# Seven-product feed-forward blocks: another order of the products, of the weight groups and of ScalarE's copies

## The chip, the cores and the metric

The kernel runs on one core of a Trainium2 chip. The metric is the device time of one execution in microseconds; the kernel before is given by the median of three runs. The engines are called as the profile calls them: PE (TensorE, matmuls), PEld (its weight loads), DVE (VectorE), ACT (ScalarE), POOL (GpSimd), and SP, whose queue issues the loads of the weights.

## The reference, cut to what matters

One inference step through two layers; 640 token columns (512 latent, 128 context) share all weights. Each layer is a half-step SwiGLU feed-forward, a mixer of three branches (state-space scan, differential attention, pooling) and a second half-step feed-forward, each with an adaptive norm. The change touches the feed-forwards and, in one point, the preparation of the scan's constants.

```python
def swiglu(h, w_in, w_out):
    a, b = jnp.split(h @ w_in, 2, axis=-1)
    return (jax.nn.silu(a) * b) @ w_out
...
    n = rmsnorm(x, ng[0]) * (1.0 + mod[..., 1, :]) + mod[..., 0, :]
    x = x + 0.5 * mod[..., 2, :] * swiglu(n, lp['w_ffn_in'][0], lp['w_ffn_out'][0])
```

The model width is 1024 (8 tiles of 128), the inner width 2816 (22 tiles).

## The kernel before, in words

Activations lie transposed, features on the partitions, and the 640 columns are two halves h = 0 and 1 of 320. Each float32 operand is split in two rounded parts, hi and lo, and a product is three matmuls (hi x hi, hi x lo, lo x hi). A weight block of 1024 x 128 is loaded raw through SP's queue into one of three buffers (`load`, L1231), cast to hi by ScalarE (L1243) and subtracted to lo by VectorE (L1244) into one of four slots.

A feed-forward (`ffn`, L1414) goes through its 22 inner tiles in parts of 5, 5, 6 and 6 (`FPARTS`). In each part every inner tile j is one unit that makes a (to which SiLU is applied) and b for both halves; then eight units of the output projection add the part to the residual. An ordinary unit has 2 halves x 2 outputs x 8 tiles of the inner dimension x 3 = 96 matmuls of 320 columns.

Three of the four feed-forwards (`fast`: the second of layer 0 and both of layer 1, called stages A, B and C here) use a seven-product scheme (`class Quad`, L65) in place of the eight half-size products of a 2 x 2 by 2 x 2 block multiplication: 7 x 4 x 3 = 84 matmuls a unit. Its weight groups are made of the two raw blocks fa and fb, each in two halves 0 and 1 of the inner dimension: GpSimd makes s1 = fb0 + fb1 (L86), s2 = s1 - fa0 (L87, both in the one buffer ws), fb0 := fa0 - fb0 (L88) and fa1 := fa1 - s2 (L89). `split` (L78) casts and splits the groups one after another: 0 is fa, 1 is ws, 2 is fb, 3 is the new fa1 (half a block, in a buffer of its own). `WHERE` says which group and half a product reads, `NEED` how many groups it wants, `FREE` where a slot is given back.

The products accumulate in three PSUM tiles. Tile x takes products 1, 6, 5 and 3, and after 1, 6 and 5 ScalarE copies it out (L124); product 6 may go into x when the copy after 1 is done, and so on. Tile w takes 7 and 4, tile y product 2. VectorE forms c11 from the copy of 1 and y (L134), c22 from the copy of 5 and w (L131), c21 from the copy of 6 and w (L141). `out` (L1461) applies SiLU to the a halves, multiplies the b halves in, and splits the result for the output projection. `steps` (L145) gives the order: 1, then 3 and 4 of the unit before, then 2, 6, 7, 5. `emit` (L1257) walks it, issues the splits as slots come free, and after products 6 and 4 runs one deferred piece (`late`) and one tick of the side jobs (`tick`).

Products 5, 6 and 7 read sums of the activations' four blocks. `combine` (L1377) forms them for k = 0 to 3, deferred at the start of a stage in two pieces of two; `combine4` (L1398) forms a last one for product 4 over the place of an activation block that ordinary units still read, so it follows them. The first part of a stage therefore starts with two ordinary units (`jj > 1`, L1470).

Side jobs run in ticks beside the main work: `mods` makes the modulation vectors from w_mod, one step per tick, and `s5_all` the scan's constants for both layers, two steps per tick during the first feed-forward of layer 0, which has 108 ticks and only ordinary units. A step ends at a `yield`; a layer has 13 + 8 x 6 = 61.

The program states an order and priorities; a scheduler then orders each engine's instructions, and each engine runs its own in order.

## Time and profile before

| | |
|---|---|
| median of three runs | 3440.04 us (3439.91 to 3443.92) |
| profiled execution, own time | 3445.12 us |
| its span | 3443.3 us |
| mean granted clock of PE | 0.976 |
| PE, DVE, ACT, POOL busy | 3236.2, 2125.9, 1316.9, 594.1 us |
| stages of the trace, us | first feed-forward 50 to 640; A 1286 to 1780; B 1780 to 2290; C 2950 to the end |

A busy share is an average over stages; which wait ends last is read from the stage. The granted clock is 1.0 at 2.4 GHz and 0.5 at 1.2 GHz. A wait is named by the instruction that waited and the one that released it; one PE group may show an idle time that another engine's queue caused. Matmuls overlap, so the pace of PE is read from the starts of successive ones, not from the duration of one.

### The profile page before, as it was taken

The page shows a single profiled execution, that of the slowest core. Times are in us where ns is not written, and L with a number is a line of the kernel's source. Part 1 is how long each engine was busy: PE and PEld are TensorE (multiplying, and loading weights), DVE is VectorE, ACT ScalarE, POOL GpSimd, SP SyncE. Part 2 cuts the span into 40 slices and gives each one's busy share as a digit, 9 for nine tenths or more (in the row PEclk, how much of TensorE's full clock was granted, in tenths as well). Part 3 has the DMA queues.
Part 4 walks back from the last instruction along what each step waited for, and adds up shares of the span by engine and source line. Part 5 has one row for each costly group of instructions (what it writes and reads, how often), then busy time and mean ns, then how long its engine had stood idle before and what let it go on. Part 6 is the DMA issues. An engine that isn't in the chain of part 4 may idle for free. (4 is left out here: it accounts for less than half of the span.)

```text
span 3443.3 us, 56364 instructions
## 1 busy us (share of the span) xinstructions
PE 3236.2 (94%) x22249; PEld 3040.6 (88%) x22249; DVE 2125.9 (62%) x4561; ACT 1316.9 (38%) x2626; POOL 594.1 (17%) x454
## 2 busy tenths in 40 slices
PE   6999999979999997999997999998999999799998
PEld 5878799979899996899996889997998999699998
DVE  4777643695785457555566545668768634855655
ACT  3333322454543234233343323345545322433432
POOL 0000000120000014323324313412000001423332
PEclk8999999989999998999998999998999999899999
DMA  6565632333213222522223652233321232122222
GB/s 206 173 222 155 212 98 70 118 114 90 87 56 130 77 86 87 165 80 83 64 88 100 192 162 80 67 117 116 98 87 56 101 102 74 43 77 75 85 68 74
DMA packets 493996, 364.55 MB, mean 106 GB/s; under 512 B 22466, under 2 KB 468260, under 8 KB 490916
## 3 DMA queue, kind: packets, MB, share of 16 engines
q1 hardware_dynamic: 463284, 311.33, 30.4%
q10 hardware_dynamic: 30448, 49.62, 4.1%
q8 instruction: 175, 2.87, 0.3%
q14 instruction: 89, 0.73, 0.1%
HBM read 327.33 MB, written 33.55 MB: 105 GB/s over the span
## 5 line engine op out<-in xcount | busy, mean ns | idle before, releaser
L1253 PE MATMUL po<-fhi,wh_fo 128*128 128x320 f32 x1408 | 443.5, 316 | 0.0
L1255 PE MATMUL po<-fhi,wl_fo 128*128 128x320 f32 x1408 | 436.1, 310 | 0.0
L1254 PE MATMUL po<-flo,wh_fo 128*128 128x320 f32 x1408 | 436.1, 310 | 0.0
L358 POOL TENSOR_TENSOR acc<-acc,sq 128x320 f32<-128x320 f32 x72 | 75.8, 1053 | 1429.5 <-ACT sq L357 1429.3
L1253 PEld LDWEIGHTS po<-fhi,wh_fo 128*128 128x128 f32 x1408 | 264.4, 188 | 28.3 <-issue 25.5
L1255 PEld LDWEIGHTS po<-fhi,wl_fo 128*128 128x128 f32 x1408 | 264.6, 188 | 2.8 <-issue 2.8
L1254 PEld LDWEIGHTS po<-flo,wh_fo 128*128 128x128 f32 x1408 | 264.8, 188 | 2.0 <-issue 1.6
L1253 PE MATMUL mg<-nhi,wh_wg 128*128 128x320 f32 x768 | 239.7, 312 | 0.0
L1255 PE MATMUL mg<-nhi,wl_wg 128*128 128x320 f32 x768 | 238.4, 310 | 0.0
L1254 PE MATMUL mg<-nlo,wh_wg 128*128 128x320 f32 x768 | 238.1, 310 | 0.0
L108 PE MATMUL qx<-thi,wh_g 128*128 128x320 f32 x480 | 156.8, 327 | 74.0 <-ACT qs L124 74.0
L86 POOL TENSOR_TENSOR ws<-wr_fb 128x512 f32<-128x512 f32 x60 | 89.4, 1489 | 743.6 <-DMA wr_fb<-in_w_ffn_in_dram 543.8
L1243 ACT CAST wh_fo<-wr_fo 128x640 fp32r<-128x640 f32 (+1 forms) x128 | 100.0, 781 | 250.6 <-PE po L1254 188.1
L1509 DVE SCALAR_TENSOR_TENSOR xT0b<-po,mod,xT0b 128x64 f32<-128x64 f32 (+1 forms) x256 | 86.8, 380 | 147.2 <-PE po L1255 147.1
L108 PEld LDWEIGHTS qx<-thi,wh_g 128*128 128x128 f32 x480 | 94.0, 196 | 84.6 <-ACT qs L124 84.6
L1244 DVE TENSOR_TENSOR wl_g<-wr_fb,wh_g 128x1024 fp32r<-128x1024 f32 x60 | 76.9, 1282 | 146.5 <-ACT wh_g L1243 146.4
L1244 DVE TENSOR_TENSOR wl_fo<-wr_fo,wh_fo 128x640 fp32r<-128x640 f32 (+1 forms) x128 | 117.2, 916 | 60.1 <-ACT wh_fo L1243 58.0
L110 PE MATMUL qx<-thi,wl_g 128*128 128x320 f32 x480 | 153.3, 319 | 0.0
L1244 DVE TENSOR_TENSOR wl_fa<-wr_fa,wh_fa 128x1024 fp32r<-128x1024 f32 x88 | 137.8, 1566 | 24.8 <-ACT wh_fa L1243 22.9
L109 PE MATMUL qx<-tlo,wh_g 128*128 128x320 f32 x480 | 152.9, 319 | 0.0
L1243 ACT CAST wh_fa<-wr_fa 128x1024 fp32r<-128x1024 f32 x88 | 92.3, 1049 | 145.5 <-PE po L1254 97.7
L1253 PEld LDWEIGHTS mg<-nhi,wh_wg 128*128 128x128 f32 x768 | 144.8, 189 | 2.3 <-issue 1.9
(531 smaller groups left out, 10233.9 us busy)
## 6 DMA issues: line engine op xcount, KB each, us to landing
wmod<-in_w_mod_dram SPq DMA_DIRECT2D x144, 512.0 KB, 4.6
wr_fa<-in_w_ffn_in_dram SPq DMA_DIRECT2D x88, 512.0 KB, 3.9
wr_fb<-in_w_ffn_in_dram SPq DMA_DIRECT2D x88, 512.0 KB, 5.7
wr_fo<-in_w_ffn_out_dram SPq DMA_DIRECT2D x64, 384.0 KB, 3.5
wr_wg<-in_w_in_dram SPq DMA_DIRECT2D x48, 512.0 KB, 4.6
wr_fo<-in_w_ffn_out_dram SPq DMA_DIRECT2D x64, 320.0 KB, 3.3
pqd<-s5pq ACTq DMA_DIRECT2D x16, 1024.0 KB, 5.2
wr_wb<-in_w_branch_dram SPq DMA_DIRECT2D x48, 256.0 KB, 2.8
```

Source lines behind the costliest of these rows:

```text
L86: T(s1, fb[:, 0:4], fb[:, 4:8], add)
L108: mm(out, a, ahi(k), start=(first and k == 0), stop=False, skip_group_check=True)
L109: mm(out, a, alo(k), start=False, stop=False, skip_group_check=True)
L110: mm(out, c, ahi(k), start=False, stop=(k == 3), skip_group_check=True)
L358: (nc.vector if k == KD - 1 else nc.gpsimd).tensor_tensor(self.acc[:, h], self.acc[:, h], sq, ALU.add)
L1243: nc.scalar.copy(hi[:, :kk], raw[:, :kk])
L1244: nc.vector.tensor_tensor(lo[:, :kk], raw[:, :kk], hi[:, :kk].bitcast(F32), ALU.subtract)
L1253: nc.tensor.matmul(out, hi[:, k], ahi(k), start=(k == 0), stop=False)
L1254: nc.tensor.matmul(out, hi[:, k], alo(k), start=False, stop=False)
L1255: nc.tensor.matmul(out, lo[:, k], ahi(k), start=False, stop=(k == kk - 1))
L1509: self.nc.vector.scalar_tensor_tensor(x, po[:, sl], gate[:, n, g : g + 1], x, ALU.mult, ALU.add)
```

## The change

The order of the products becomes 1, 7, 3 of the unit before, 6, 4 of the unit before, 2, 5; group 1 is now fb and group 2 ws; c11 lies in another buffer and its SiLU is issued with product 3; the deferred pieces and ticks follow products 6 and 5. The first part of a stage has four ordinary units and one seven-product unit, `combine` is deferred in four pieces, and one of the additions of `combine4` moves from GpSimd to VectorE. The scan's preparation has one step less per eighth of a layer and runs one step per tick.

```diff
--- before.py
+++ after.py
@@ -67,10 +67,10 @@
 
 
 
-    NEED = {1: 1, 2: 1, 6: 2, 7: 3, 5: 3, 3: 4, 4: 4}
-    FREE = {1: 0, 2: 1, 6: 0, 7: 0, 5: 1, 3: 0, 4: 1}
-
-    WHERE = {1: (0, 0), 2: (0, 1), 6: (1, 0), 5: (1, 1), 7: (2, 0), 4: (2, 1), 3: (3, 0)}
+    NEED = {1: 1, 7: 2, 6: 3, 2: 3, 5: 3, 3: 4, 4: 4}
+    FREE = {1: 0, 7: 0, 6: 0, 2: 1, 5: 1, 3: 0, 4: 1}
+
+    WHERE = {1: (0, 0), 2: (0, 1), 7: (1, 0), 4: (1, 1), 6: (2, 0), 5: (2, 1), 3: (3, 0)}
 
     def __init__(self, build, name, blocks, acts, out):
         self.b, self.name, self.blocks, self.acts, self.out = build, name, blocks, acts, out
@@ -89,9 +89,9 @@
             T(fa[:, 4:8], fa[:, 4:8], s2, sub)
             return r
         if g == 1:
-            return b.split((None, 8, f"g2{self.name}"), self.s)
+            return b.split((None, 8, f"g2{self.name}"), fb)
         if g == 2:
-            return b.split((None, 8, f"g3{self.name}"), fb)
+            return b.split((None, 8, f"g3{self.name}"), self.s)
         hi = b.tq.tile([P, 4, P], F32R, tag="whi4", name=f"whg4{self.name}", bufs=1)
         lo = b.tq.tile([P, 4, P], F32R, tag="wlo4", name=f"wlg4{self.name}", bufs=1)
         b.nc.scalar.copy(hi, fa[:, 4:8])
@@ -130,12 +130,12 @@
                 self.c22 = b.tq.tile([P, HT], F32, tag="tt", name=f"c22{nm}", bufs=2)
                 V.tensor_tensor(self.c22, t, self.w, ALU.add)
         elif p == 2:
-            self.c11 = b.tp.tile([P, HT], F32, tag="sq", name=f"c11{nm}")
+            self.c11 = b.tp.tile([P, HT], F32, tag="sa", name=f"c11{nm}")
             V.tensor_tensor(self.c11, self.s1, self.y, ALU.add)
-            self.out(0, 0, self.c11)
         elif p == 3:
             self.out(0, 1, self.x)
             self.out(1, 1, self.c22)
+            self.out(0, 0, self.c11)
         elif p == 4:
             c21 = b.tq.tile([P, HT], F32, tag="tt", name=f"c21{nm}", bufs=2)
             V.tensor_tensor(c21, self.u2, self.w, ALU.add)
@@ -144,11 +144,13 @@
     @staticmethod
     def steps(quads):
 
-        st, before = [], []
+
+        st, old = [], None
         for q in quads:
-            st += [(q, 1)] + before + [(q, p) for p in (2, 6, 7, 5)]
-            before = [(q, 3), (q, 4)]
-        return st + before
+            st += [(q, 1), (q, 7)] + ([(old, 3)] if old else []) + [(q, 6)] + ([(old, 4)] if old else [])
+            st += [(q, 2), (q, 5)]
+            old = q
+        return st + ([(old, 3), (old, 4)] if old else [])
 
 
 class Build:
@@ -682,7 +684,6 @@
             V.tensor_tensor(qv[0], cr, wr, ALU.mult)
             V.tensor_tensor(tmp, ci, wi, ALU.mult)
             V.tensor_tensor(qv[0], qv[0], tmp, ALU.add)
-            yield
             V.tensor_tensor(qv[1], ci, wr, ALU.mult)
             V.tensor_tensor(tmp, cr, wi, ALU.mult)
             V.tensor_tensor(qv[1], qv[1], tmp, ALU.subtract)
@@ -1320,7 +1321,7 @@
                 cnt["fourth"] -= h == 3
                 if u.FREE[h] or h == 3:
                     fill()
-                if h in (6, 4):
+                if h in (6, 5):
                     self.late()
                     self.tick()
                 continue
@@ -1396,11 +1397,11 @@
         self.put(self.thi[:, 2, k], self.tlo[:, 2, k], t3)
 
     def combine4(self, k, name):
-        Q = self.nc.gpsimd
+        Q, V = self.nc.gpsimd, self.nc.vector
         t = self.tq.tile([P, HT], F32, tag="tt", name=f"t3{k}{name}", bufs=2)
         e = self.tp.tile([P, HT], F32, tag="nt", name=f"e{k}{name}")
         Q.tensor_tensor(t, self.nhi[:, 4 + k, 0].bitcast(F32), self.nlo[:, 4 + k, 0].bitcast(F32), ALU.add)
-        Q.tensor_tensor(e, self.thi[:, 1, k].bitcast(F32), self.tlo[:, 1, k].bitcast(F32), ALU.add)
+        V.tensor_tensor(e, self.thi[:, 1, k].bitcast(F32), self.tlo[:, 1, k].bitcast(F32), ALU.add)
         Q.tensor_tensor(t, t, e, ALU.subtract)
         self.put(self.nhi[:, k, 1], self.nlo[:, k, 1], t)
 
@@ -1429,8 +1430,8 @@
                         self.tq = self.open("tq", bufs=1)
                         self.thi = self.tq.tile([P, 3, 4, HT], F32R, name=f"thi{l}{i}")
                         self.tlo = self.tq.tile([P, 3, 4, HT], F32R, name=f"tlo{l}{i}")
-                        for k in (0, 2):
-                            self.deferred.append((2, lambda k=k: [self.combine(x, f"{l}{i}") for x in (k, k + 1)]))
+                        for k in range(4):
+                            self.deferred.append((2, lambda k=k: self.combine(k, f"{l}{i}")))
                 f["hi"] = self.hp.tile([P, FW, 2, HT], F32R, tag="fhi", name=f"fhi{l}{i}{q}")
                 f["lo"] = self.hp.tile([P, FW, 2, HT], F32R, tag="flo", name=f"flo{l}{i}{q}")
 
@@ -1467,7 +1468,7 @@
                     nc.vector.tensor_tensor(sa[h], sa[h], x, ALU.mult)
                     self.put(f["hi"][:, jj, h], f["lo"][:, jj, h], sa[h])
 
-                if fast and (q > 0 or jj > 1):
+                if fast and (q > 0 or jj > 3):
                     quads.append(Quad(self, f"{l}{i}{j}", blocks, self.nacts, out))
                 else:
                     ins.append((blocks, run))
@@ -1653,7 +1654,7 @@
                     left = [y for y in left if y is not g]
         self.close("io", "wm")
         self.bp = self.open("bp", bufs=2)
-        self.sides.append((self.s5_all(), 2, SDB))
+        self.sides.append((self.s5_all(), 1, SDB))
         for l in range(DEPTH):
 
             def begin(l=l):
```

ScalarE in stage A, one unit of a steady stretch. wh_g are casts of weight groups (g2 the second, g3 the third, g4 the fourth), wh_fa that of the first; qs1, qs6 and qs5 are the copies of x after products 1, 6 and 5; c11 and sa take SiLU, fhi are outputs. Before:

```order
L1243 CAST wh_g2018_14969<-ws_018_14944 128x1024
L1464 ACTIVATE c11017_14966<-c11017_14966 128x320
L124 COPY qs6017_14985<-qx017_14889 128x320
L1243 CAST wh_g3018_15016<-wr_fb018_14887 128x1024
L124 COPY qs5017_15012<-qx017_14889 128x320
L124 COPY qs1018_15035<-qx018_15022 128x320
L97 CAST whg4018_15054<-wr_fa018_14792 128x512
L1464 ACTIVATE sa0171_15049<-qx017_14889 128x320
L902 CAST fhi011_14670<-sa0171_15049 128x320
L1243 CAST wh_fa019_15078<-wr_fa019_14925 128x1024
L902 CAST fhi011_14670<-c11017_14966 128x320
```

Now:

```order
L1244 CAST wh_g2018_14973<-wr_fb018_14864 128x1024
L1465 ACTIVATE c11017_14971<-c11017_14971 128x320
L1244 CAST wh_g3018_14993<-ws_018_14949 128x1024
L124 COPY qs5017_14989<-qx017_14866 128x320
L124 COPY qs1018_15012<-qx018_14999 128x320
L97 CAST whg4018_15045<-wr_fa018_14783 128x512
L1465 ACTIVATE sa0171_15039<-qx017_14866 128x320
L903 CAST fhi011_14648<-sa0171_15039 128x320
L124 COPY qs6018_15063<-qx018_14999 128x320
L1244 CAST wh_fa019_15083<-wr_fa019_14916 128x1024
L903 CAST fhi011_14648<-c11017_14971 128x320
```

The copy after product 6 has moved ahead of the casts of the next unit's groups; these stand between the cast of the old unit's output and the copy after product 5, fb first.

GpSimd at the start of stage A, from the third weight sum of the last unit in the first part on; e, t are the terms of `combine4`. Before:

```order
L1403 TENSOR_TENSOR e101_13768<-thi01_13326,tlo01_13327 128x320
L1402 TENSOR_TENSOR t3001_13760<-nhi_82,nlo_83 128x320
L1404 TENSOR_TENSOR t3001_13760<-t3001_13760,e001_13761 128x320
L1403 TENSOR_TENSOR e201_13775<-thi01_13326,tlo01_13327 128x320
L89 TENSOR_TENSOR wr_fa013_13314<-wr_fa013_13314,ws_013_13751 128x512
L1402 TENSOR_TENSOR t3101_13767<-nhi_82,nlo_83 128x320
L1404 TENSOR_TENSOR t3101_13767<-t3101_13767,e101_13768 128x320
L1403 TENSOR_TENSOR e301_13782<-thi01_13326,tlo01_13327 128x320
L1402 TENSOR_TENSOR t3201_13774<-nhi_82,nlo_83 128x320
L1404 TENSOR_TENSOR t3201_13774<-t3201_13774,e201_13775 128x320
L1402 TENSOR_TENSOR t3301_13781<-nhi_82,nlo_83 128x320
L1404 TENSOR_TENSOR t3301_13781<-t3301_13781,e301_13782 128x320
```

Now:

```order
L88 TENSOR_TENSOR wr_fb014_13706<-wr_fa014_13621,wr_fb014_13706 128x512
L1403 TENSOR_TENSOR t3001_14025<-nhi_82,nlo_83 128x320
L1403 TENSOR_TENSOR t3101_14032<-nhi_82,nlo_83 128x320
L1405 TENSOR_TENSOR t3001_14025<-t3001_14025,e001_14026 128x320
L1405 TENSOR_TENSOR t3101_14032<-t3101_14032,e101_14033 128x320
L89 TENSOR_TENSOR wr_fa014_13621<-wr_fa014_13621,ws_014_13872 128x512
L1403 TENSOR_TENSOR t3201_14039<-nhi_82,nlo_83 128x320
L1405 TENSOR_TENSOR t3201_14039<-t3201_14039,e201_14040 128x320
L1403 TENSOR_TENSOR t3301_14046<-nhi_82,nlo_83 128x320
L1405 TENSOR_TENSOR t3301_14046<-t3301_14046,e301_14047 128x320
```

The additions e are gone from GpSimd, and all weight sums but one of the part's only seven-product unit stand ahead of the terms t.

## Rows read from the trace of the kernel before

**Rows 1.** The page, busy us (share of the span) and instructions of each engine.

```profile
PE 3236.2 (94%) x22249; PEld 3040.6 (88%) x22249; DVE 2125.9 (62%) x4561; ACT 1316.9 (38%) x2626; POOL 594.1 (17%) x454
```

**Rows 2.** Waits on PE, whole span: us in total, times, longest us.

```profile
PE qx L108 <- ACT qs L124: 74.0, 37, 7.9
PE mps L282 <- DMA wmod<-in_w_mod_dram: 21.8, 16, 2.8
```

**Rows 3.** Stretches: length, PE, PEld, DVE, ACT, POOL busy (x), PEclk, DMA share, GB/s.

```profile
1310.00:1370.00 60.00, 42.54 (x250) 36.24 (x248) 40.78 (x51) 20.92 (x41) 33.61 (x25) 0.80 0.29 87
1362.00:1780.00 418.00, 401.02 (x2728) 386.15 (x2728) 237.85 (x388) 149.94 (x250) 122.86 (x79) 0.99 0.33 97
1820.00:1880.00 60.00, 41.15 (x249) 36.52 (x248) 37.07 (x54) 19.75 (x38) 30.80 (x23) 0.83 0.33 100
2960.00:3020.00 60.00, 36.20 (x189) 32.49 (x188) 40.18 (x54) 22.45 (x42) 35.81 (x27) 0.77 0.11 32
3020.00:3400.00 380.00, 362.48 (x2419) 357.63 (x2418) 224.49 (x341) 141.78 (x237) 115.92 (x72) 0.99 0.27 79
```

**Rows 4.** Waits on PE behind the starts: 1362 to 1780, 1870 to 2290, 3020 to 3400.

```profile
PE qx L108 <- ACT qs L124: 16.5, 11, 2.2
...
PE qx L108 <- ACT qs L124: 12.1, 9, 1.8
...
PE qx L108 <- ACT qs L124: 17.5, 11, 2.2
```

**Rows 5.** Timeline of PE in stage A: start us, us, instruction, [idle before <-releaser].

```profile
1456.73 0.31 PE L108 MATMUL qx<-thi,wh_g 128*128 128x320 f32 x1
...
1458.49 0.31 PE L108 MATMUL qw<-thi,wh_g 128*128 128x320 f32 x1
...
1461.69 0.41 PE L108 MATMUL qx<-thi,wh_g 128*128 128x320 f32 x1 [1.28 <-ACT qs L124]
```

**Rows 6.** Timeline of ACT there.

```profile
1456.51 0.46 ACT L902 CAST fhi<-c 128x320 fp32r<-128x320 f32 x1
1459.91 1.05 ACT L1243 CAST wh_g<-ws 128x1024 fp32r<-128x1024 f32 x1 [2.93 <-POOL ws L87]
1460.86 0.47 ACT L1464 ACTIVATE c<-c 128x320 f32<-128x320 f32 x1
1461.23 0.41 ACT L124 COPY qs<-qx 128x320 f32<-128x320 f32 x1
```

**Rows 7.** Timelines of DVE and of the SP queue there.

```profile
1450.87 1.23 DVE L1244 TENSOR_TENSOR wl_g<-wr_fb,wh_g 128x1024 fp32r<-128x1024 f32 x1 [2.30 <-ACT wh_g L1243]
...
1452.12 0.37 SPq L1234 DMA_DIRECT2D wr_fb<-in_w_ffn_in_dram  x1
...
1456.53 2.18 DVE L1244 TENSOR_TENSOR wl_fa<-wr_fa,wh_fa 128x1024 fp32r<-128x1024 f32 x1
...
1460.14 0.47 DVE L134 TENSOR_TENSOR c<-qs,qy 128x320 f32<-128x320 f32 x1
```

**Rows 8.** Timeline of POOL: the last column sum of A's start, and the weight sums there.

```profile
1341.82 1.00 POOL L1404 TENSOR_TENSOR t<-t,e 128x320 f32<-128x320 f32 x1
...
1456.14 1.50 POOL L86 TENSOR_TENSOR ws<-wr_fb 128x512 f32<-128x512 f32 x1 [6.41 <-DVE flo L903]
1457.71 2.16 POOL L87 TENSOR_TENSOR ws<-ws,wr_fa 128x512 f32<-128x512 f32 x1
1459.83 1.52 POOL L88 TENSOR_TENSOR wr_fb<-wr_fa,wr_fb 128x512 f32<-128x512 f32 x1
```

**Rows 9.** First feed-forward, 50 to 640: the stretch, and groups of DVE (busy, mean ns).

```profile
50.00:640.00 590.00, 573.13 (x4116) 515.31 (x4117) 362.58 (x886) 192.29 (x348) 14.37 (x14) 0.98 0.48 151
...
L1509 DVE SCALAR_TENSOR_TENSOR xT<-po,mod,xT 128x64 f32<-128x64 f32 x126 | 43.7, 379 | 55.9 <-PE po L1255 55.8
L1244 DVE TENSOR_TENSOR wl_fo<-wr_fo,wh_fo 128x640 fp32r<-128x640 f32 (+1 forms) x32 | 28.4, 890 | 13.7 <-ACT wh_fo L1243 13.1
L716 DVE TENSOR_TENSOR s5ba<-s5ba,s5tmp 128x512 f32<-128x512 f32 x32 | 22.0, 687 | 0.3
```

## The prediction

> **What bounds the kernel.** The engine table comes first: TensorE is busy 94% of the span, ScalarE 38%, GpSimd 17% [rows 1]. Time is therefore gained only where TensorE stands idle or runs at its lower clock, or by giving it fewer matmuls. The list of waits then says who stops it: the largest entry is the matmul at line 108 that waits for the ScalarE copy at line 124, 74.0 us in 37 waits, then loads of the modulation weights [rows 2]. Those lines run only in the three feed-forward stages with the seven-product form (A, B and C, whose starts lie at 1310, 1820 and 2960 us). The table of stretches splits their loss in two. At each start 60 us hold 42.5, 41.2 and 36.2 us of TensorE work at a mean clock of 0.80, 0.83 and 0.77 [rows 3]: 17.5 + 18.9 + 23.8 = 60.1 us idle, and 2 x (1 - clock) x 60 = 24.0 + 20.4 + 27.6 = 72 us at 1.2 GHz instead of 2.4. Behind the starts the same wait returns 11, 9 and 11 times, 16.5 + 12.1 + 17.5 = 46.1 us [rows 4], with a clock of 0.99 in A and C [rows 3].
>
> One such wait in order of time. Product 6 ended when product 7 began, at 1458.49, and product 5 may start when ScalarE has copied product 6 out. It starts at 1461.69 [rows 5]. ScalarE takes its instructions one after another: ahead of that copy stand the cast of the weight sums (it waited 2.93 us for GpSimd) and a SiLU, and the copy itself runs from 1461.23 [rows 6]. The cast waits for a chain that begins with the buffer of the second raw block: its split ends at 1450.87 + 1.23 = 1452.10, the DMA into it is issued at 1452.12 [rows 7], GpSimd's first sum starts at 1456.14 (4.0 us later) and its second ends at 1459.87 [rows 8]. So a late sum blocks a copy that has nothing to do with it, because only product 7 stood between 6 and 5.
>
> **The change, part by part.** *Order of products.* Steady state becomes 1, 7, 3 of the old unit, 6, 4 of the old unit, 2, 5; no product is added or lost. One product is 12 matmuls and takes 1458.49 - 1456.73 = 1.76 us, 0.1467 us a matmul [rows 5]; seven take 12.32 us, and I count from the start of product 1. Each pair that shares the accumulator x now has two products between: 1 (ends 1.76) to 6 (starts 5.28), 6 (7.04) to 5 (10.56), 5 (12.32) to 3 (15.84). The copy after 6 stands on ScalarE behind a cast of the old unit's output and takes 0.41 us [rows 6]: done by 8, 2.5 us early. The cast of the sums now stands after product 5, whose end frees its weight slot: 12.4 to 13.45, then the copy of 5 until 13.9, 1.9 us early. The SiLU of c11 moves one step later, between two casts; its product is wanted only after product 4 of the next period. Raw blocks are loaded in the same order through the same queue, and GpSimd keeps its four sums per unit. So all 46.1 us have their reason removed.
>
> What is late next? Product 7 now comes second, at 14.08, and needs the weight group from the second raw block. Its slot is freed by product 2 at 10.56; cast 1.05 us from 10.8; then the split on VectorE, behind the addition after product 2 (0.47) and for 1.23 us when alone [rows 7], to 13.1. Its third matmul, the first that reads the split, is due at 14.4: 1.3 us early. The loop also closes: split done 13.1, DMA 4.0, three sums 1.50 + 2.16 + 1.52 [rows 8], in all 22.3, or 10.0 in the next period against the cast at 10.8. Margins of 0.8 and 1.3 us are thin. A split that meets GpSimd took 2.18 us instead of 1.23 [rows 7], so I leave 0.2 us at each change of unit inside a block (4 + 5 + 5 per stage, 42 in all), 8 us; the ends are 0 and 1.4 us each (about a whole sum, 1.5), 0 to 59.
>
> VectorE's 2.18 us beside GpSimd, and 0.47 us beside it for the addition that reads one side from PSUM [rows 7], show the pattern. The Trainium skill ("SBUF — State Buffer", Who interferes with whom) states it as a lock: a VectorE operation with two SBUF inputs and a GpSimd operation that reads SBUF exclude each other for a whole instruction. By that rule the split for product 7 can wait out a full sum at every unit, and the time would be 3386 instead of 3335; the trace agrees on the lock, not yet on where it bites here.
>
> *Two more ordinary units in the first block.* Two units of 84 matmuls become two of 96 in each of three blocks: 72 matmuls x 0.1467 = +10.6 us, all on TensorE and so on the path. In return the first seven-product unit starts 2 x 96 x 0.1467 = 28 us later. GpSimd's last column sum in A ended at 1341.82 + 1.00 [rows 8], 33 us into the stretch of rows 3. Of the starts' 60.1 us, 74.0 - 46.1 = 27.9 are copies behind the casts of those sums [rows 2, 4], the rest products that wait for sums, weight splits or a modulation load, with VectorE busy 40.8 of 60 us [rows 3]. With 28 us of independent matmuls ahead, products 1, 7, 6, 2, 5 and 3 (10.6 us) also pass before product 4 wants the last sum. I leave 2 us of 20 per block: 6 of the 60.1 (ends 0 and half, 30). As this block has a single seven-product unit, product 3 follows 5 directly, filled only by a few small matmuls: I add 1 us per block, 3 (ends 0 and the longest steady wait, 2.2 us each, 7) [rows 4].
>
> *The clock.* Of the 72 us at half clock some was idle. Lost time is (72 - 60.1) / 2 = 6 us if all idle time fell in it, 36 if none; I take 19, near the middle, and 6 of the 0.01 x (418 + 380) = 8 us in the steady parts of A and C [rows 3]. With the waits gone 4 of these 25 stay.
>
> *Column sums in four steps, one addition moved from GpSimd to VectorE, buffer of c11, ticks at 5 instead of 4.* Same work in smaller pieces beside TensorE; twelve additions, each near the 0.47 us of the one in rows 7, change engine under 28 us of cover. Nothing; without the cover they are part of the 30 above.
>
> *S5 preparation at half the rate.* Until 640 us the preparation ran two steps per tick; its 61 steps a layer become 53, one per tick: 106 of the 108 ticks of this feed-forward, where it was over half-way. TensorE idles 16.9 us there [rows 9], mostly waiting for modulation loads queued behind it [rows 2]. Halved density relieves the first half. The last stretch of 16 ticks lasts 16 x 18 x 0.1467 = 42 us, and VectorE then has 16 x 0.76 residual adds, 8 x 0.89 splits and 3.2 groups of twelve operations of 0.687 [rows 9]: 46 us, so 4 us spill before the norm. Ends: -17 and +5; I take -5.
>
> **Sum.** Own time of the profiled execution 3445.1: +10.6 - 46 + 8 - 60 + 6 + 3 - 25 + 4 - 5 = -104.5, about 3340.5. That execution lies 5.1 us over the median 3440.0 of the runs, so on their scale **3335**.
>
> **Rivals.** *Product 7's weights late through GpSimd:* the split waits out a sum at each of 42 unit changes. For it: rows 7 and the thin margins; against: the sums mostly fall earlier in the period. 42 x 1.4 = 59 instead of 8: 3386.
>
> *The copies still blocked:* ScalarE's new row order has other casts ahead of the copy of 5, and the steady waits stay: 46 instead of 8, and the clock's 6: 3379. Against: the slack above.
>
> *The starts do not shrink:* ordinary units need two full splits each, on a VectorE that the sums already fill, and half of the idle time moves into them: 30 instead of 6, and 9 of clock: 3368.
>
> *Slower:* the place is the buffer of the second raw block. If its DMA must wait for the buffer of the other block (freed only after product 3, near 6.7 of the period) rather than its own, the data lands at 10.7, three sums end at 15.9, cast and split at 18.2, where product 7 wants it at 14.4: 3.9 us in each of 42 changes, +164 - 8: about 3491. It decides from (3440 - 3335 + 8) / 42 = 2.7 us a unit. Against: the DMA followed its own split by 0.02 us [rows 7].
>
> *No change at all:* the scheduler undoes the order; the rows of the change on ScalarE speak against it. 3440.
>
> **How the numbers follow.** Forecast 0.73, product 7 late 0.12, copies blocked 0.06, starts 0.05, slower 0.03, none 0.01. Low end: no residue (21) and 12 more from the S5 part, 3302. High end: product 7 late at 3386, which takes the second and third rival in: 3387. No change means within 0.2%, 7 us, about what a measurement of this kernel can tell. Faster 0.95, same 0.01, slower 0.04.
>
> **What would show it.** Right: line 108's wait for the copy of line 124 falls from 74 us to below 10; clock near 1 at the starts; 54 instead of 60 first sums. Wrong: waits of w products (lines 108, 110) for the split or GpSimd at every unit, or stretches after 1310 still at 0.8.

## The result, and the profile after

| | before | after |
|---|---|---|
| median of the runs | 3439.97 us (4 runs) | **3333.99 us** (3330.81 to 3337.91, 4 runs) |
| ratio | | 0.969, 95% interval 0.9674 to 0.9707 |
| profiled execution, own time and span | 3445.12, 3443.3 us | 3330.81, 3329.0 us |

The forecast of 3335 us is met, 1 us from the median. Whether its steps are met is another question, and the rest of this document is about that. Medians and ratios here and below are of executions at the normal clock; a single one, of the kernel "S5 alone" below, ran in a slower state (3619.4 us at a granted clock of 0.832) and is left out.

The engine line of the page of after, against [rows 1]:

```profile
PE 3213.5 (97%) x22321; PEld 3028.1 (91%) x22321; DVE 2124.0 (64%) x4543; ACT 1291.7 (39%) x2596; POOL 494.8 (15%) x418
```

TensorE has the 72 matmuls more that were counted (22321 against 22249), and is busy 97% instead of 94%. The waits on PE of after, whole span (us in total, times, longest), against [rows 2]:

```profile
PE qw L110 <- DVE wl_g L1245: 16.7, 29, 0.6
...
PE mps L284 <- DMA wmod<-in_w_mod_dram: 9.2, 11, 1.8
...
PE qx L108 <- ACT qs L124: 7.6, 2, 5.5
```

The wait for the copies fell from 74.0 us in 37 waits to 7.6 in 2, both at starts (B and C). A new entry leads: product 7 waits for the split of its weights, 29 times. Stretches of after, begun within 2 us of the same distance behind the first norm of a stage as those of [rows 3], in the same columns:

```profile
1290.00:1350.00 60.00, 60.00 (x442) 53.31 (x441) 43.88 (x70) 21.40 (x41) 22.18 (x16) 1.00 0.51 156
1350.00:1726.00 376.00, 369.55 (x2511) 356.56 (x2510) 227.90 (x355) 138.04 (x230) 107.59 (x79) 1.00 0.32 95
1766.00:1826.00 60.00, 57.88 (x416) 50.94 (x414) 39.41 (x67) 19.18 (x38) 18.31 (x16) 0.97 0.48 146
...
2880.00:2940.00 60.00, 54.50 (x353) 53.70 (x352) 46.56 (x71) 23.40 (x46) 21.23 (x18) 0.94 0.22 66
```

The 60 us at the starts now hold 60.0, 57.9 and 54.5 us of TensorE work (42.5, 41.2 and 36.2 before) at a clock of 1.00, 0.97 and 0.94 (0.80, 0.83 and 0.77). In A the same 60 us hold 442 matmuls instead of 250.

The new wait in order of time. Timeline of PE in after, stage A (the unit's product 2, the first three matmuls of products 1 and 7 in part, product 2 of the next unit):

```profile
1516.20 0.31 PE L108 MATMUL qy<-nhi,wh_fa 128*128 128x320 f32 x1
...
1519.87 0.31 PE L109 MATMUL qx<-nlo,wh_fa 128*128 128x320 f32 x1
1520.30 0.42 PE L110 MATMUL qx<-nhi,wl_fa 128*128 128x320 f32 x1
...
1522.02 0.31 PE L109 MATMUL qw<-tlo,wh_g 128*128 128x320 f32 x1
1522.93 0.41 PE L110 MATMUL qw<-thi,wl_g 128*128 128x320 f32 x1 [0.60 <-DVE wl_g L1245]
...
1529.78 0.31 PE L108 MATMUL qy<-nhi,wh_fa 128*128 128x320 f32 x1
```

Timeline of DVE and of POOL there:

```profile
1519.02 1.22 DVE L1245 TENSOR_TENSOR wl_fa<-wr_fa,wh_fa 128x1024 fp32r<-128x1024 f32 x1
1520.16 0.48 DVE L904 TENSOR_TENSOR flo<-c,fhi 128x320 fp32r<-128x320 f32 x1
1520.56 0.48 DVE L134 TENSOR_TENSOR c<-qs,qy 128x320 f32<-128x320 f32 x1
1520.96 1.92 DVE L1245 TENSOR_TENSOR wl_g<-wr_fb,wh_g 128x1024 fp32r<-128x1024 f32 x1
...
1520.39 1.41 POOL L89 TENSOR_TENSOR wr_fa<-wr_fa,ws 128x512 f32<-128x512 f32 x1 [2.55 <-DVE wl_fa L1245]
```

GpSimd's fourth sum (line 89) overwrites half of fa, so it starts when VectorE has split fa, at 1520.39, and ends at 1521.80. VectorE's split for product 7 starts at 1520.96, beside it, and takes 1.92 us. Product 7's third matmul, due 0.147 us after 1522.02, starts at 1522.93. That split also starts late, as the timeline of ACT there shows:

```profile
1517.40 1.05 ACT L1244 CAST wh_fa<-wr_fa 128x1024 fp32r<-128x1024 f32 x1
1519.14 0.46 ACT L903 CAST fhi<-c 128x320 fp32r<-128x320 f32 x1 [0.69 <-DVE c L1468]
1519.51 1.05 ACT L1244 CAST wh_g<-wr_fb 128x1024 fp32r<-128x1024 f32 x1
```

Product 2 ended, and freed the slot, 1.76 us behind 1516.20, at 1517.96. The cast for product 7 starts 1.55 us after that, because in ScalarE's row it stands behind the cast of an output of the old unit, which waited for VectorE. Even 1.22 us of split would then have ended at 1522.18, just when the matmul was due.

Note how the two views of TensorE differ: the list counts 0.60 us for this wait, the starts show 0.76 (a matmul's end is modelled, and its 0.31 us covers part of the gap); product 1's third matmul is 0.28 us late (1520.30 for 1520.02) without any entry. The distance from product 2 to product 2 is the safe measure: 13.58 us here, where the seven products need 12.32. Before it was 13.88, as the timeline of PE in before shows:

```profile
1441.09 0.31 PE L108 MATMUL qy<-nhi,wh_fa 128*128 128x320 f32 x1
...
1454.97 0.31 PE L108 MATMUL qy<-nhi,wh_fa 128*128 128x320 f32 x1
```

So in this pair of units the new order won only 0.30 of 1.56 us. Summed over the 42 distances inside the second, third and fourth parts of the three stages it is more: 584.2 us before, 554.3 after, where the seven products alone need 517.4. That is 30 of the 106 us, and where the rest came from had to be found by taking the change apart.

### The profile page after: what moved, and what is told of

Its sections match the earlier page's. It is cut to its first block, busy times and chain, and to the rows that moved or that the text cites. A ratio compares the mean times of both kernels' runs of the same rounds, so it can differ in the third digit from the quotient of the medians.

```text
span 3329.0 us, 56455 instructions
## 1 busy us (share of the span) xinstructions
PE 3213.5 (97%) x22321; PEld 3028.1 (91%) x22321; DVE 2124.0 (64%) x4543; ACT 1291.7 (39%) x2596; POOL 494.8 (15%) x418
## 4 chain that ended last, share of the span: by engine, by line
PE 75%; DVE 15%; issue 4%; ACT 3%; DMA 3%; POOL 0%; DVEq 0%; ACTq 0%; SPq 0%; POOLq 0%
PE po L1254 6%; PE po L1255 6%; PE po L1256 6%; PE mg L1254 3%; PE mg L1256 3%; PE mg L1255 3%; PE qx L108 2%; PE qx L109 2%; PE pa L1254 2%; PE mps L284 2%; PE qx L110 2%; PE pa L1255 2%; PE pa L1256 2%; PE pb L1255 2%; PE pb L1254 2%
## 5 line engine op out<-in xcount | busy, mean ns | idle before, releaser
L1254 PE MATMUL pa<-nhi,wh_fa 128*128 128x320 f32 x544 | 173.2, 319 | 1.0 <-ACT nhi L422 1.0
L1255 PE MATMUL pa<-nlo,wh_fa 128*128 128x320 f32 x544 | 168.1, 312 | 1.2 <-DVE nlo L423 1.1
L1256 PE MATMUL pa<-nhi,wl_fa 128*128 128x320 f32 x544 | 168.5, 310 | 0.0
L1256 PE MATMUL pb<-nhi,wl_fb 128*128 128x320 f32 x544 | 168.4, 310 | 0.0
L1255 PE MATMUL pb<-nlo,wh_fb 128*128 128x320 f32 x544 | 168.3, 309 | 0.0
L1254 PE MATMUL pb<-nhi,wh_fb 128*128 128x320 f32 x544 | 168.2, 309 | 0.0
L86 POOL TENSOR_TENSOR ws<-wr_fb 128x512 f32<-128x512 f32 x54 | 73.9, 1368 | 624.5 <-DMA wr_fb<-in_w_ffn_in_dram 529.2
L1255 PEld LDWEIGHTS mg<-nlo,wh_wg 128*128 128x128 f32 x768 | 144.3, 188 | 0.5 <-issue 0.5
```

The lines of the kernel that those rows point to most:

```text
L86: T(s1, fb[:, 0:4], fb[:, 4:8], add)
L1254: nc.tensor.matmul(out, hi[:, k], ahi(k), start=(k == 0), stop=False)
L1255: nc.tensor.matmul(out, hi[:, k], alo(k), start=False, stop=False)
L1256: nc.tensor.matmul(out, lo[:, k], ahi(k), start=False, stop=(k == kk - 1))
```

## Experiments: the three parts alone

**Order alone** (the kernel before with the new `NEED`, `FREE`, `WHERE`, `split`, `run`, `steps` and ticks), **ordinary units alone**, **S5 alone**, and **the change without S5**. Of their edits these lines matter; the first fence is against the kernel after (that run also keeps the old column sums and the old step of S5), the other two against the kernel before; the change without S5 is the kernel after with the third edit undone:

```diff
-                if fast and (q > 0 or jj > 3):
+                if fast and (q > 0 or jj > 1):
...
-        self.sides.append((self.s5_all(), 1, SDB))
+        self.sides.append((self.s5_all(), 2, SDB))
```
```diff
-        Q.tensor_tensor(e, self.thi[:, 1, k].bitcast(F32), self.tlo[:, 1, k].bitcast(F32), ALU.add)
+        V.tensor_tensor(e, self.thi[:, 1, k].bitcast(F32), self.tlo[:, 1, k].bitcast(F32), ALU.add)
...
-                        for k in (0, 2):
...
+                        for k in range(4):
...
-                if fast and (q > 0 or jj > 1):
+                if fast and (q > 0 or jj > 3):
```
```diff
-            yield
             V.tensor_tensor(qv[1], ci, wr, ALU.mult)
...
-        self.sides.append((self.s5_all(), 2, SDB))
+        self.sides.append((self.s5_all(), 1, SDB))
```

> The kernel before with only the new order of products, weight groups, c11 and ticks (two ordinary units, old combine, S5 preparation as before). Theory, parts add up: the 46 us of steady waits at line 108 go, some 16 us of waits for product 7's split come (in after 29 waits, 16.7 us), and a little clock returns behind the starts; the starts keep most of their 60 us idle. Expected 3440 - 46 + 16 - 6 = about 3404 (3390 to 3415). Rival: the order alone also clears the starts, because the 27.9 us of copies there stood behind the casts of sums as in the steady state; then 3404 - 28 - 15 of clock = about 3360, and the ordinary units are worth little.

> The kernel before with only four ordinary units, column sums in four steps and one addition on VectorE; the order of the products stays. Theory: 10.6 us of matmuls more, of the starts' 60 us idle some 50 less, of the clock some 15 less; the steady waits at line 108 stay (about 46 us): 3440 + 10.6 - 50 - 15 = about 3385 (3375 to 3400). Rival: with the old order the copies at the start still stand behind casts of sums, so that the 27.9 us of them stay: about 3413 to 3425.

> The kernel before with only the S5 preparation at half its rate (and its one step less). As predicted this was worth 5 us: 3435. Theory after reading the two traces: from the first norm to the next the first feed-forward fell from 593.33 to 575.58 us, so 18 us, and the kernel alone with this edit takes about 3422 (3417 to 3426). Rival: part of the 18 us comes from the load at the start of the kernel and not from the rate, then 3428 to 3436.

> The changed kernel with the S5 preparation as before (two steps per tick). Theory: the parts add up and this one is worth 18 us: 3334 + 18 = 3352 (3348 to 3356). By the term of the prediction (5 us): 3339. If order and ordinary units overlap, the gain of this kernel over the kernel before differs from the sum of the gains of the two runs with one part alone by over 10 us.

| run | median, us | ratio to before (95%) | gain of 3440, us | first feed-forward, A, B, C in the trace, us |
|---|---|---|---|---|
| before | 3440 | | | 593.3, 509.0, 515.9, 515.5 |
| order alone | 3406.8 | 0.9901 (0.9881 to 0.9922) | 34 (27 to 41) | 593.4, 494.6, 508.7, 502.3 |
| ordinary units alone | 3371.1 | 0.9802 (0.9777 to 0.9827) | 68 (60 to 77) | 588.5, 480.5, 496.9, 492.8 |
| S5 alone | 3431.5 | 0.997 (0.995 to 0.999) | 10 (3 to 17) | 581.9, 504.0, 519.0, 513.4 |
| the change without S5 | 3343.8 | 0.9718 (0.9695 to 0.9741) | 97 (89 to 105) | 596.0, 475.0, 488.8, 479.4 |
| the change | 3334.0 | 0.969 (0.9674 to 0.9707) | 107 (101 to 112) | 575.6, 473.8, 489.5, 481.9 |

(A stage runs from the first matmul of its norm's spread, tile rb_x in the first feed-forward and rb_n behind it, to that of the next norm, C to the end of the span.) The parts add up within the intervals: 34 + 68 + 10 = 112 against 107, and 34 + 68 = 102 against 97. The theory held for the order (3404 expected). The ordinary units gave more than the 55 expected, and end 4 us under the expected range; their rival (copies at the start stay blocked, 3413 or more) is out. S5 lies between the two guesses, at 10, by both runs, with an interval of 3 to 17. The traces tell the same: in the six of all runs of this document with the old rate the first feed-forward took 588.5 to 596.0 us (mean 592.1), in the eight with the new one 575.6 to 583.2 (mean 580.1), while the mixer behind it took 2.4 us more (635.2 against 632.8). The 18 us that I read from the first pair of traces were partly the luck of two executions.

## Experiments: product 7's weights

In **half split** the split that product 7 reads becomes two operations; the other kernel leaves out the **fourth sum**, so that its last weight group is a plain half of fa.

```diff
         if g == 1:
-            return b.split((None, 8, f"g2{self.name}"), fb)
+            hi = b.wp.tile([P, KW, P], F32R, tag="whi", name=f"wh_g2{self.name}", bufs=SPL)
+            lo = b.wp.tile([P, KW, P], F32R, tag="wlo", name=f"wl_g2{self.name}", bufs=SPL)
+            b.nc.scalar.copy(hi, fb)
+            for c in (slice(0, 4), slice(4, 8)):
+                b.nc.vector.tensor_tensor(lo[:, c], fb[:, c], hi[:, c].bitcast(F32), sub)
+            return hi, lo
```
```diff
             T(fb[:, 0:4], fa[:, 0:4], fb[:, 0:4], sub)
-            T(fa[:, 4:8], fa[:, 4:8], s2, sub)
```

> The changed kernel with the split of the second weight group (the one product 7 reads) issued as two VectorE operations of 128x512 in place of one of 128x1024; product 7 reads only the first half. Theory: the 16.7 us in 29 waits are the end of an operation of which product 7 wants the first half; they fall below 3 us, and the time by about 14 us, to 3320 (3315 to 3326). Rival, the chain shifts: one operation more per unit on VectorE delays the copies and splits behind it, or the first half still waits for GpSimd's sum as long as the whole: waits of 10 us or more stay, 3330 to 3338.

> The changed kernel without GpSimd's fourth sum (line 89); it leaves out the subtraction fa1 - s2, so the last weight group is a plain half of fa. Theory: this sum runs beside the split that product 7 wants (1.92 us instead of 1.23) and is what makes it late; without it the split takes about 1.23 us, the waits at line 110 fall from 16.7 to below 4 us, 3320 (3315 to 3327). Rival: the split is late because its cast and the additions ahead of it on VectorE are; then it takes 1.23 to 1.5 us, the waits stay above 8 us and the time above 3328.

Half split: 3311.5 us, ratio 0.9632 (0.9606 to 0.9657). No fourth sum: 3309.8 us, ratio 0.9625 (0.9604 to 0.9646). In both, the entry of line 110 for the split is gone from the waits, and both gained more, 22 and 24 us, than the 14 us that were expected from the 16.7 us in the list. Instructions of the tile wl_g (ns: min, median, max), in after and without the fourth sum:

```profile
L1245 DVE TENSOR_TENSOR wl_g<-wr_fb,wh_g x54: 1210/1917/1935, 1317.1 to 3251.0; 128x1024 fp32r<-128x1024 f32 x54
L1245 DVE TENSOR_TENSOR wl_g<-ws,wh_g x54: 1208/1212/1227, 1320.6 to 3252.8; 128x1024 fp32r<-128x1024 f32 x54
```
```profile
L1244 DVE TENSOR_TENSOR wl_g<-wr_fb,wh_g x54: 1210/1219/1894, 1320.7 to 3231.5; 128x1024 fp32r<-128x1024 f32 x54
```

Same operation, same shape: 1917 ns beside the fourth sum, 1219 without it. The rival (late by its cast and the additions ahead) would have left the waits; it falls as the cause of them. But cast and additions had used up the margin: over the 42 changes of unit in after the cast starts 1.1 us (median) behind the end of product 2, and 0.1 to 0.2 us at the first change of each part; without the fourth sum the split ends, in the median, 0.1 us before its matmul is due. Half split keeps the sum, and the meeting is seen in its timeline of DVE, POOL and PE:

```profile
1520.94 0.47 DVE L139 TENSOR_TENSOR c<-qs,qy 128x320 f32<-128x320 f32 x1
1521.34 1.98 DVE L96 TENSOR_TENSOR wl_g<-wr_fb,wh_g 128x512 fp32r<-128x512 f32 x2
...
1520.77 1.41 POOL L89 TENSOR_TENSOR wr_fa<-wr_fa,ws 128x512 f32<-128x512 f32 x1 [1.63 <-DVE wl_fa L1250]
...
1517.05 0.31 PE L113 MATMUL qy<-nhi,wh_fa 128*128 128x320 f32 x1
...
1522.47 0.31 PE L114 MATMUL qw<-tlo,wh_g 128*128 128x320 f32 x1
1522.78 0.42 PE L115 MATMUL qw<-thi,wl_g 128*128 128x320 f32 x1
...
1529.63 0.31 PE L113 MATMUL qy<-nhi,wh_fa 128*128 128x320 f32 x1
```

The two halves still take 1.98 us together, so the collision is the same, but product 7's third matmul reads the first half only: it is 0.16 us late instead of 0.76, and the distance is 12.58. Summed over the 42 distances: 554.3 us in after, 529.9 with the half split. What the half split takes away of the lateness of product 7's weights is thus 24 us. **Half split beats both kernels, and of the kernels here that do the whole computation none is faster**; its gain over after is 0.6% (the two intervals do not touch).

## Experiments: why the copies were late before

The prediction said that a late sum blocks the copy. So, in the kernel before, the cast of the second group reads fa; all sums are still made, but this kernel leaves them out of that group's products. Then, on top of that, c11 is formed from the copy of product 6 instead of that of product 1, so that its SiLU stands behind this copy; the copy of 1 goes into nothing.

```diff
         if g == 1:
-            T(fa[:, 4:8], fa[:, 4:8], s2, sub)
...
-            return b.split((None, 8, f"g2{self.name}"), self.s)
+            return b.split((None, 8, f"g2{self.name}"), fa)
...
+        T(fa[:, 4:8], fa[:, 4:8], self.s[:, 0:4], sub)
         hi = b.tq.tile([P, 4, P], F32R, tag="whi4", name=f"whg4{self.name}", bufs=1)
```
```diff
                 self.u2 = t
+                self.c11 = b.tp.tile([P, HT], F32, tag="sq", name=f"c11{nm}")
+                V.tensor_tensor(self.c11, self.u2, self.y, ALU.add)
+                self.out(0, 0, self.c11)
...
-        elif p == 2:
-            self.c11 = b.tp.tile([P, HT], F32, tag="sq", name=f"c11{nm}")
-            V.tensor_tensor(self.c11, self.s1, self.y, ALU.add)
-            self.out(0, 0, self.c11)
```

> The kernel before, old order of everything, but the second weight group is cast from the raw block fa instead of GpSimd's sums; it leaves the sums out of that group's product, though GpSimd still makes them (the fourth one a little later). Theory: the steady waits at line 108 come from a cast that waits for GpSimd and holds up the copy behind it on ScalarE; with a source that is there early 40 of the 46 us go without any other order, and some of the 28 us of copies at the starts: 3440 - 40 - 10 = about 3390 (3370 to 3402). Rival: one product between 6 and 5 is too little for a copy behind any cast; then over 25 us of the steady waits stay, and the time is above 3415.

> The kernel of the run before on this point (old order, second weight group cast from fa), and c11 formed from the copy of product 6 instead of the copy of product 1, so that its SiLU stands behind that copy on ScalarE and not ahead of it; the copy of 1 goes into nothing. Theory, mended: ScalarE held the copy back twice, first by the cast that waits for GpSimd's sum, behind it by the SiLU of c11 that waits for VectorE's addition; with both out of the way the 37 us of steady waits that the first edit left at line 108 fall below 8 us, and the time to 3421 - 30 - 5 = about 3385 (3377 to 3396). Rival: with one product between 6 and 5 the copy is too late whatever stands ahead of it on ScalarE; then over 20 us of these waits stay and the time is 3405 or more.

Without the wait for the sum: 3420.9 us, ratio 0.9947 (0.9931 to 0.9964). My theory missed: 37.0 of the 46.1 us of [rows 4] stayed. Both signs of the rival came true (over 25 us stay, time above 3415), but not its reason, as the second edit shows. The waits behind the starts of A, B and C:

```profile
PE qx L108 <- ACT qs L124: 15.4, 11, 2.3
...
PE qx L108 <- ACT qs L124: 7.1, 9, 1.2
...
PE qx L108 <- ACT qs L124: 14.5, 11, 2.2
```

Its timelines of PE, ACT and DVE say why (product 6 ends at 1452.32, product 7 1.76 us later, product 5 starts at 1455.38):

```profile
1455.38 0.42 PE L108 MATMUL qx<-thi,wh_g 128*128 128x320 f32 x1 [1.14 <-ACT qs L124]
...
1450.71 1.05 ACT L1243 CAST wh_g<-wr_fa 128x1024 fp32r<-128x1024 f32 x1
1454.54 0.47 ACT L1464 ACTIVATE c<-c 128x320 f32<-128x320 f32 x1 [2.79 <-DVE c L134]
1454.92 0.41 ACT L124 COPY qs<-qx 128x320 f32<-128x320 f32 x1
...
1450.37 2.18 DVE L1244 TENSOR_TENSOR wl_fa<-wr_fa,wh_fa 128x1024 fp32r<-128x1024 f32 x1
1452.47 1.57 DVE L903 TENSOR_TENSOR flo<-c,fhi 128x320 fp32r<-128x320 f32 x1
1453.97 0.47 DVE L134 TENSOR_TENSOR c<-qs,qy 128x320 f32<-128x320 f32 x1
```

The cast now runs early, at 1450.71, but the next in ScalarE's row is the SiLU of c11. It waits 2.79 us for VectorE's addition, which stands behind two operations that GpSimd's sums stretch (2.18 and 1.57 us). In [rows 6] that SiLU stood in the shadow of the cast. With it behind the copy too: 3403.8 us, ratio 0.9905 (0.9879 to 0.9931). Timelines of ACT and PE (first matmuls of products 7 and 5) of that kernel:

```profile
1448.08 0.43 ACT L124 COPY qs<-qx 128x320 f32<-128x320 f32 x1 [0.82 <-PE qx L110]
1452.22 0.47 ACT L1463 ACTIVATE c<-c 128x320 f32<-128x320 f32 x1 [3.71 <-DVE c L130]
1452.60 1.03 ACT L1242 CAST wh_g<-wr_fb 128x1024 fp32r<-128x1024 f32 x1
1453.54 0.74 ACT L124 COPY qs<-qx 128x320 f32<-128x320 f32 x2
...
1447.83 0.31 PE L108 MATMUL qw<-thi,wh_g 128*128 128x320 f32 x1
...
1449.59 0.31 PE L108 MATMUL qx<-thi,wh_g 128*128 128x320 f32 x1
```

The copy after product 6 now waits for the matmul alone (0.82 us), and product 5 follows product 7 without a gap (1.76 us), in the old order of the products. So the one product between 6 and 5 was enough; the row on ScalarE was the cause. But the SiLU and the cast behind it now hold the copy after product 5, and product 3 waits: 7.0 + 4.4 + 7.6 = 19.0 us stay, and the time, 3403.8, is between theory and rival. In the three orders of ScalarE's row tried with the old order of products something stood ahead of one of the copies each time; in the new one each copy has two products of time, and in the steady parts no copy is listed as a wait any more.

## Experiments: the start of a stage

**Three ordinary units** (`jj > 2`), **column sums as before**, and two with the half split: the **cast of the last column sums on VectorE**, alone and with three units. The first fence is column sums as before, the second the cast.

```diff
-        V.tensor_tensor(e, self.thi[:, 1, k].bitcast(F32), self.tlo[:, 1, k].bitcast(F32), ALU.add)
+        Q.tensor_tensor(e, self.thi[:, 1, k].bitcast(F32), self.tlo[:, 1, k].bitcast(F32), ALU.add)
...
-                        for k in range(4):
-                            self.deferred.append((2, lambda k=k: self.combine(k, f"{l}{i}")))
+                        for k in (0, 2):
+                            self.deferred.append((2, lambda k=k: [self.combine(x, f"{l}{i}") for x in (k, k + 1)]))
```
```diff
-        self.put(self.nhi[:, k, 1], self.nlo[:, k, 1], t)
+        V.tensor_copy(self.nhi[:, k, 1], t)
+        V.tensor_tensor(self.nlo[:, k, 1], t, self.nhi[:, k, 1].bitcast(F32), ALU.subtract)
```

> The changed kernel with three ordinary units at the start of a stage in place of four. Theory: with the new order the starts have cover to spare (stage A has no wait over 0.3 us before 1400), so that each stage saves 12 matmuls, 3 x 12 x 0.1467 = 5.3 us, and gives back one more unit change with 0.5 us of waits: 3334 - 5 + 2 = 3331 (3326 to 3336). Rival: the fourth unit is what covers the last column sums; without it products 6, 5 or 4 wait 5 to 8 us per stage and the clock falls with them: 3350 to 3365.

> The changed kernel with the column sums in two pieces and all additions of the last sum on GpSimd, as before. The prediction put this part at nothing: 3334 (3330 to 3339), the waits at the starts as in the changed kernel. Rival: the last sums on GpSimd end 8 x 0.5 us later with one seven-product unit waiting for them, and the two remaining start waits (2.1 us in B, 5.5 us in C) become 5 us or more in each stage: 3342 to 3355.

> The kernel with the half split, and the cast of the last column sums (four 128x320 pieces a stage, line 903 by way of combine4) on VectorE instead of ScalarE. Theory: the two start waits that are left (2.1 us in B, 5.1 us in C) are copies that stand on ScalarE behind those casts while they wait for GpSimd; they go, and with them some clock: 3311.5 - 9 = about 3303 (3300 to 3308). Rival: VectorE is as late as ScalarE, the wait takes another name, 3309 to 3318.

> The kernel with the half split and the cast of the last column sums on VectorE, and three ordinary units in place of four. Theory: with three units the copy of product 1 waited 7 to 12 us a stage behind such a cast; without it 5 us of matmuls are saved and a few us of waits for the sums themselves come: 3305 (3298 to 3315). Rival: the column sums themselves are too late for product 7 or 4, whatever the engine of the cast, and the waits of 5 to 12 us a stage stay: 3320 to 3345.

| run | median, us | ratio to before (95%) | A, B, C in the trace, us |
|---|---|---|---|
| three ordinary units | 3367.8 | 0.9793 (0.9771 to 0.9814) | 486.7, 501.7, 486.2 |
| column sums as before | 3342.8 | 0.9721 (0.9699 to 0.9743) | 477.3, 491.8, 481.8 |
| half split | 3311.5 | 0.9632 (0.9606 to 0.9657) | 465.2, 481.8, 471.7 |
| and cast on VectorE | 3312.1 | 0.9633 (0.9619 to 0.9648) | 465.6, 484.4, 471.7 |
| and three ordinary units | 3345.4 | 0.9726 (0.971 to 0.9743) | 477.9, 496.6, 477.5 |

One ordinary unit less saves 5.3 us of matmuls, and yet the kernel takes 33 to 34 us more, with or without the half split: the fourth unit is needed. The wait that returns, in the waits on PE with three units, first with the casts as in after, then with them on VectorE:

```profile
PE qx L108 <- ACT qs L124: 31.3, 3, 12.1
```
```profile
PE qx L113 <- ACT qs L129: 29.1, 3, 10.9
```

One copy a stage, 7 to 12 us late. My theory, that it stands behind the casts of the column sums on ScalarE, fell: with those casts on VectorE 29.1 us of the same wait stay, and the time does not change with four units either. The timelines of ACT and POOL of the last run (three units, cast on VectorE) show what the copy waits for:

```profile
1324.50 0.46 ACT L1459 CAST fhi<-sa 128x320 fp32r<-128x320 f32 x1 [4.62 <-DVE sa L1458]
1329.48 0.42 ACT L129 COPY qs<-qx 128x320 f32<-128x320 f32 x1 [4.51 <-POOL t L1410]
...
1327.44 0.94 POOL L1408 TENSOR_TENSOR t<-nhi,nlo 128x320 f32<-128x320 f32 x1
1328.46 0.99 POOL L1410 TENSOR_TENSOR t<-t,e 128x320 f32<-128x320 f32 x1
```

ScalarE is idle for 4.51 us and the copy starts when GpSimd's subtraction t - e ends (1328.46 + 0.99 = 1329.45). The copy's target (`run`, tag "nt") and e (`combine4`, tag "nt") share the two buffers of one tag, so I read this as the copy waiting for the buffer of e. A tag of its own for e, which would show it, was not tried. Column sums as before cost 5.7 us in A, B and C by the traces (8.8 by the medians, with an interval that overlaps that of after).

## Why the prediction was right, by its steps

- **The bound** was read rightly: every gain found is TensorE's idle time or clock in A, B, C and the first feed-forward.
- **Order of products** (-46, +8, and -2 of clock net: -40): 34 measured (27 to 41). The steady waits for copies went, as said, but both terms were too small. The waits of 46.1 us come from the list, which understates: the 42 distances took 579.6 to 584.2 us in three traces with the old order (before, ordinary units alone, S5 alone) and 529.9 with the new order and the half split, so 50 to 54 us could go. And the 8 us for product 7's weights (0.2 us at each change of unit) are 24, by the half split.
- **The step that failed** is that margin for product 7, "1.3 us early". At the first change of each part it was there: the cast started 0.1 to 0.2 us behind the end of product 2, and the split was done 1.4 us or more before it was due. Later the cast starts up to 1.6 us behind that end, since ScalarE's and VectorE's rows put work of the old unit ahead of cast and split; the prediction put 0.24 us there. The fourth sum, which is released by the split of fa and so runs beside the next split, I left out; it adds the 0.7 us by which the matmul is late. The first rival had the collision, listed at 29 of 42 changes, with a price of about 0.8 us instead of 1.4.
- By the distances the order is thus worth 26 to 30 us behind the starts. In the pair of traces before and order alone, A, B and C fell by 34.8 us: 30 in the 42 distances (584.2 to 553.9), most of the rest ahead of the second part of each stage.
- By the Trainium skill ("SBUF — State Buffer", Who interferes with whom) VectorE's operation with two SBUF inputs and GpSimd's read of SBUF contend. The trace agrees, in nearly full waits: the 128x512 half begun at 1521.34 beside a sum that ended 0.84 us later, at 1522.18, took 1.38 us instead of 0.68.
- **That "a late sum blocks a copy"** was half of the cause: behind the cast the SiLU of c11 held the same copy nearly as long. The forecast did not hang on it, since the change moves both.
- **Ordinary units** (+10.6, -60, +6, +3, -19 of clock: -59): 68 measured (60 to 77). The cover of 28 us was judged rightly, and is not generous: with 14 it fails. In after 7.6 us of copies' waits are left at the starts, where 6 and 3 were forecast to stay idle. What the clock alone gave back no run separates; at the starts it rose from 0.80, 0.83 and 0.77 to 1.00, 0.97 and 0.94.
- **Column sums in four steps: "nothing".** About 6 us by the traces of one execution each; the medians' intervals overlap. They belong to the cover.
- **S5** (-5, ends -17 and +5): 10 (3 to 17). The waits for modulation loads fell, as the step said: 16.7 to 21.8 us in the six traces with the old rate, 9.2 to 14.0 in the eight with the new one.
- So the sum is right in part by luck, because errors met: inside the order a larger gain met a larger loss and left 6 us less than forecast; the ordinary units gave 9 more, S5 5 more, and all together 5 less than apart, 107 where 104.5 were forecast. Of these differences only that of the ordinary units lies outside its interval. The range, 3302 to 3387, takes in each of these errors alone.

## What to carry to other kernels

Where an engine runs its row in order, list everything that stands ahead of the instruction another engine needs, with what each of them waits for: removing the first blocker may only show the second. Where the row cannot be cleared, give a result that TensorE waits for more time (two products instead of one here), and split a weight preparation where its first reader needs only half. Check a margin not in the first round of a loop but in the later ones: here it was there in the first round of each part and gone from the second on. Measure a loop by the distance between starts: the list of waits here named 16.7 us where 24 could be had, and 46.1 where 50 to 54 could.

## What the runs showed of the hardware that was not expected

GpSimd's 128x512 sum of 1.41 us lengthens VectorE's 128x1024 split from 1.22 to 1.92 us; over the 42 changes of unit, where a product waits for that split, leaving the sum out or halving the split wins 22 to 24 us, though VectorE is busy 64% and GpSimd 15%. An addition that reads one side from PSUM took 0.47 us within the same sum (1520.94 in the half split). TensorE's listed idle time understates short waits: 0.60 us listed, 0.76 by the starts, and 0.28 us in the same unit not listed at all. The Trainium skill ("Perfetto Trace Analysis", Tensor Engine Instruction) says that a matmul's end is estimated, not observed; this agrees.
